# Seven products in shared PSUM banks, and an issue order written down for four engines

## The chip, the cores and the metric

The program runs on one core of a Trainium2 chip. A core has a matrix engine (TensorE, PE in the profile, with its weight loads as PEld), a vector engine (VectorE, DVE), an activation engine (ScalarE, ACT), a general engine (GpSimd, POOL) and an engine that here issues the DMAs (SyncE, SP). Each takes its instructions from a queue of its own, in order, and the engines wait for each other through semaphores. SBUF is the working memory, PSUM the eight banks that matmuls write to; POOL has no instruction here that reads PSUM.

The metric is the time of one execution on the device, in microseconds (us), lower being better.

## The reference

Two transformer-like layers over 512 latent tokens and 256 context tokens, width 1024. Each layer mixes tokens (layer 0: gated linear attention and a chunk MLP, layer 1: attention and a Fourier mix) and then runs a gated feed-forward block. Only this block matters for the change:

```python
def conv_ffn(h, w_up, conv_w, conv_b, w_down):
    t_len = h.shape[1]
    up = h @ w_up                                   # 1024 -> 2 x 2816
    gate, val = up[..., :D_FF], up[..., D_FF:]
    pad = CONV_W // 2
    gp = jnp.pad(gate, ((0, 0), (pad, pad), (0, 0)))
    gate_c = conv_b
    for j in range(CONV_W):                         # 3 taps along the tokens
        gate_c = gate_c + gp[:, j:j + t_len] * conv_w[j]
    return (jax.nn.silu(gate_c) * val) @ w_down
...
xl = xl + g2 * conv_ffn(modulate(xl, norm_ffn_w[l], sh2, sc2), ffn_w_up[l], ...)
```

In layer 0 it runs over latent and context tokens (768 columns), in layer 1 over the latent ones (512). All in float32.

## The kernel before

Features lie on the partitions, tokens in the columns. A float32 operand is kept as two tiles: `h`, the value rounded to the matmul's format by a cast on ACT, and `l`, the rest, from one subtraction on DVE or POOL. A product of two such pairs takes three matmuls (`mm3`, L499 to L503).

**Tiles and stages.** The hidden width 2816 is 22 tiles of 128. A tile needs 128 gate and 128 value features. Its result (`acts[i]`) goes into the second matrix product, "down", which runs in groups of tiles: layer 0 has groups of 3, 3, 3, 3, 3, 3, 4 tiles, layer 1 of 2, 4, 4, 4, 4, 4. In layer 0 the whole "down" of a group follows the first tile of the next group (24 x 6 matmuls of 512 or 256 columns). In layer 1 it is cut into chunks, one behind each tile (24 matmuls of 512 columns in the steady state, two output columns `m`). The last group's "down" follows all tiles (`down_last`). The first two tiles of a layer are computed plainly; tiles 2 to 21 by *products*.

**Products.** The tile's 2 x 2 block product (gate and value weights, each in two halves of the inner dimension, by the inputs, each in two halves of the tokens `n1` and `n2`) is made by seven products p0 to p6 instead of eight, each 12 matmuls of half the tokens: 384 columns in layer 0, 256 in layer 1. Their recombination is

- gate, first half: g1 = p0 + p5
- gate, second half: g2 = p0 + p1 + p3 + p2
- value, first half: u = p0 + p1 + p4 + p6
- value, second half: w = p0 + p1 + p3 + p4

Before, each product goes into a PSUM bank alone, and DVE makes one copy and seven adds out of PSUM (L1145 to L1162). There are eight banks under two tags, "mm" and "aux", four each; a tile takes two of each and uses three of them twice.

**Tail.** From gate, u and w: bias and middle tap (ACT, L1172, "bias step"), two shifted multiply-adds on DVE per token segment (L1174, L1176, "shifts"; layer 0 has two segments, so four), Silu (ACT, L1178), multiplication by u (POOL, L1179) and by w (DVE, L1180), then the pair for "down": cast (ACT, L1182) and subtraction (POOL, L1183). "Down" ends with the residual, one DVE instruction per segment that reads PSUM (L990).

**The weight stream** (`_Stream`, L292). Raw weights come by DMA on SP's queue. A unit of the look-ahead (`prep`) makes the pairs: for a plain or "down" chunk one cast (L490) and one subtraction (L492; POOL for most chunks); for a tile of products five units. Product 0, 5 and 6 take a raw quarter, 1, 2 and 3 need three sums on DVE first (L381 to L383), 4 one (L387); then a cast on ACT (L390) and a subtraction (L392) each, on DVE for the products in `PROD_ON_V`, else on POOL. `next`, called ahead of each product and each "down" chunk, emits the units that fit:

```python
def ready(self):
    ...
    own = PROD_OWN[int(self.order[i][0][2:])]
    return used + len([j for j in u if j not in own]) <= 6 and not self.own & set(u)

def next(self, key):
    ...                                  # the item before is no longer live
    while key not in self.hl:
        self.prep()
    while self.ready():
        self.prep()
    ...
```

Six tiles of the pool `whl` hold the prepared weights: one for a product, two for a "down" chunk; the products in `PROD_OWN` have buffers of another pool. Three buffers (tag "t2k") hold u, w and the sum for product 4; in layer 0 three others (tag "ada") hold gate, t1 and product 6's weights.

**What sets the order.** The framework's scheduler: it takes the instructions of all engines from a heap, by priorities and a planned time, and decides each engine's order as well as which buffer a tile gets. So the order in which the code emits is not the order in which an engine issues.

Of the kernel before, what the change touches and what calls it, by code (L numbers as in the profile page):

```python
# [11 lines left out]
F32 = mybir.dt.float32  # L12
# [4 lines left out]
ALU = mybir.AluOpType  # L17
# [32 lines left out]


def prod_order(layer, t):

    return PROD_FIRST if t == FF_PLAIN[layer] else PROD_USE

# [236 lines left out]
class _Stream:  # L292
# [4 lines left out]
    def __init__(self, nc, w, raw_pool, hl_pool, order, offs, split, last_pool, sums):  # L297
# [6 lines left out]
        while i < len(order):  # L304
            kind, t = order[i]
            if kind[:2] == "up" and FF_PLAIN[int(kind[2:])] <= t < NFF:
                for u in PROD_UNITS:
                    self.units.append((i, u))
                self.items += [(kind, t, j) for j in prod_order(int(kind[2:]), t)]
# [111 lines left out]
def backbone(ctx: ExitStack, tc, w, xt, ada, vec, cst, msk, rop, wst, bs, pew, out):  # L421
# [77 lines left out]
    def mm3(ps, a, b, first, last):  # L499

        T.matmul(ps, a[0], b[0], start=first, stop=False)  # L501
        T.matmul(ps, a[0], b[1], start=False, stop=False)  # L502
        T.matmul(ps, a[1], b[0], start=False, stop=last)  # L503


    bg = {"gla": deque(), "ada": deque(), "sum": deque()}
# [485 lines left out]
    def out_pass(key, nk, src, dst, gcol, each, chunks=None):  # L992

        per = 8 // nk
        for m in range(KD):
# [5 lines left out]
            ps = [bank("mm") for _ in d]  # L1001
# [24 lines left out]
    def ffn(layer, X, src, parts, late, down_last):  # L1026
# [106 lines left out]
        def up_products(t, gate):  # L1133
# [4 lines left out]
            def product(j, ps):  # L1138
                h, l = ws.next((f"up{layer}", t, j))
                for kk in range(4):  # L1140
                    mm3(ps[:, 0:nh], (h[:, kk * P:(kk + 1) * P], l[:, kk * P:(kk + 1) * P]), rhs[j][kk],
                        kk == 0, kk == 3)
                return ps[:, 0:nh]

            def add(o, a, b):  # L1145
                V.tensor_tensor(o, a, b, op=ALU.add)  # L1146

            b1, b2, b4, b3 = bank("mm"), bank("mm"), bank("aux"), bank("aux")
            u = tp.tile([P, nh], F32, tag="t2k", name="u")
            w_ = tp.tile([P, nh], F32, tag="t2k", name="w")  # L1150
            g1, g2, u, w_ = gate[:, n1], gate[:, n2], u[:], w_[:]
            todo = [((0,), lambda p: V.tensor_copy(g1, p[0])), ((0, 1), lambda p: add(u, g1, p[1])),
                    ((1, 3), lambda p: add(w_, u, p[3])), ((2, 3), lambda p: add(g2, w_, p[2])),
                    ((3, 4), lambda p: add(u, u, p[4])), ((3, 4), lambda p: add(w_, w_, p[4])),
                    ((1, 5), lambda p: add(g1, g1, p[5])), ((3, 4, 6), lambda p: add(u, u, p[6]))]
            banks = (b1, b2, b4, b3, b1, b2, b3)
            done = {}
# [639 lines left out]
```

## Time and profile before

| what | value |
|---|---|
| time, median of 3 runs | 1715.54 us (1711.6 to 1715.75) |
| the profiled execution's own time | 1715.11 us |
| its span, first to last instruction | 1713.3 us |
| PE busy | 1609.6 us (94%) |
| DVE busy | 1160.7 us (68%) |
| ACT busy | 684.8 us (40%) |
| POOL busy | 736.5 us (43%) |
| granted PE clock, mean | 0.989 |
| layer 0, tiles by products | 507 to 972 us |
| layer 1, tiles by products | 1354 to 1690 us |

The profile is of one execution. In a row of a group, the numbers are busy time in us, mean ns of one instruction, and the idle time of the engine before them with what ended it. A row of the waits has engine, line and releaser, then us in total, times and the longest. A row of the timeline has start, length, engine, line, and what it wrote and read. Names such as wp, kt, lt, slot and t are those of the program's tiles: wp is a product's prepared weight, wh and wl are those of a chunk, kt, lt and slot are pools. Matmuls overlap, so the distance between their starts is what one costs.

### The profile page before, as it was taken

To read this page: it belongs to the slowest core of one execution; us is meant where nothing else is said; L and a number is where in the kernel's file an instruction comes from. 1 tells how busy PE (TensorE), PEld (TensorE's weight loads), DVE (VectorE), ACT (ScalarE), POOL (GpSimd) and SP (SyncE) were. 2 spreads that over 40 slices of the span, in tenths; PEclk is the share of its full clock that TensorE was granted. 3 is DMA by queue.
4 is the path that set the end of the run, shared out by engine and by line. 5 is a ranking of instruction groups with operands and counts; after the bars stand their busy time and mean duration, and the time that the engine had idled before them with its cause. 6 is when DMAs were issued, how large, how long until landed. Compare 5 with 4: busy or idle time off the path is not lost.

```text
span 1713.3 us, 28274 instructions
## 1 busy us (share of the span) xinstructions
PE 1609.6 (94%) x11130; PEld 1423.2 (83%) x11130; DVE 1160.7 (68%) x2125; ACT 684.8 (40%) x1373; POOL 736.5 (43%) x456
## 2 busy tenths in 40 slices
PE   5999999989999999999999999989899989999999
PEld 4777777778999989889898888666799978888887
DVE  5337676752756756666566784777866788888884
ACT  4323333522453323233232453556654544343431
POOL 1221223344535656565565423411126355555551
PEclk9999999999999999999999999999999999999999
DMA  9353434323412122121221223633015222222222
GB/s 365 98 190 119 150 112 141 119 88 109 136 35 77 53 69 77 59 77 47 73 79 58 81 84 104 243 119 106 18 52 170 82 74 91 89 97 87 99 78 83
DMA packets 53205, 175.11 MB, mean 102 GB/s; under 512 B 5712, under 2 KB 7760, under 8 KB 53072
## 3 DMA queue, kind: packets, MB, share of 16 engines
q1 hardware_dynamic: 52208, 172.24, 30.8%
q8 instruction: 88, 1.44, 0.3%
q10 hardware_dynamic: 864, 1.07, 0.2%
q14 instruction: 45, 0.37, 0.1%
HBM read 171.18 MB, written 2.10 MB: 101 GB/s over the span
## 4 chain that ended last, share of the span: by engine, by line
PE 61%; DVE 21%; issue 5%; POOL 5%; ACT 4%; DMA 3%; ACTq 0%; DVEq 0%; SPq 0%; POOLq 0%
PE mm L501 14%; PE mm L502 14%; PE mm L503 14%; PE aux L501 3%; PE aux L502 3%; PE aux L503 3%; DVE wp L392 3%; PE aux L572 2%; POOL wl L492 2%; DMA raw<-in_w_dram 1%; DVE qk L832 1%; POOL wp L392 1%; DVE qk L830 1%; DVE kt L382 1%; PE aux L1105 1%
## 5 line engine op out<-in xcount | busy, mean ns | idle before, releaser
L492 POOL TENSOR_TENSOR wl<-raw,wh 128x1024 fp32r<-128x1024 f32 (+6 forms) x143 | 311.9, 2183 | 503.0 <-ACT wh L490 452.1
L490 ACT CAST wh<-raw 128x1024 fp32r<-128x1024 f32 (+5 forms) x155 | 146.4, 945 | 145.4 <-PE mm L502 75.9
L392 POOL TENSOR_TENSOR wp<-sum,wp 128x512 fp32r<-128x512 f32 x80 | 111.7, 1403 | 155.7 <-ACT wp L390 155.7
L501 PE MATMUL mm<-slot,wh 128*128 128x512 f32 (+1 forms) x480 | 163.7, 342 | 12.7 <-DVE xl L990 10.8
L502 PE MATMUL mm<-slot,wh 128*128 128x512 f32 (+1 forms) x480 | 163.0, 340 | 1.0 <-POOL slot L1183 0.7
L503 PE MATMUL mm<-slot,wl 128*128 128x512 f32 (+1 forms) x480 | 162.1, 338 | 0.0
L990 DVE SCALAR_TENSOR_TENSOR xl<-mm,mods,xl 128x512 f32<-128x512 f32 (+1 forms) x128 | 90.9, 712 | 96.9 <-PE mm L503 96.6
L392 POOL TENSOR_TENSOR wp<-raw,wp 128x512 fp32r<-128x512 f32 x80 | 113.7, 1429 | 67.5 <-ACT wp L390 67.5
L501 PE MATMUL mm<-xt,wh 128*128 128x256 f32 (+1 forms) x384 | 135.1, 354 | 0.2 <-ACT xt L641 0.2
L390 ACT CAST wp<-sum 128x512 fp32r<-128x512 f32 x100 | 60.8, 620 | 185.6 <-DVE sum L387 79.7
L502 PE MATMUL mm<-xt,wh 128*128 128x512 f32 (+1 forms) x384 | 129.8, 339 | 0.0
L503 PE MATMUL mm<-xt,wl 128*128 128x512 f32 (+1 forms) x384 | 129.7, 339 | 0.0
L501 PEld LDWEIGHTS mm<-slot,wh 128*128 128x128 f32 x480 | 90.7, 189 | 26.8 <-DVE xl L990 12.0
L501 PE MATMUL mm<-lt,wh 128*128 128x512 f32 (+2 forms) x308 | 107.1, 348 | 0.0
L503 PE MATMUL mm<-lt,wl 128*128 128x512 f32 (+2 forms) x308 | 106.6, 346 | 0.0
L502 PE MATMUL mm<-lt,wh 128*128 128x512 f32 (+2 forms) x308 | 106.6, 346 | 0.0
L502 PEld LDWEIGHTS mm<-slot,wh 128*128 128x128 f32 x480 | 91.1, 190 | 11.6 <-POOL slot L1183 1.1
L503 PEld LDWEIGHTS mm<-slot,wl 128*128 128x128 f32 x480 | 91.2, 190 | 10.4
L390 ACT CAST wp<-raw 128x512 fp32r<-128x512 f32 x100 | 61.8, 618 | 95.0 <-PE mm L502 36.5
L501 PEld LDWEIGHTS mm<-xt,wh 128*128 128x128 f32 x384 | 72.3, 189 | 26.3 <-issue 16.8
L1179 POOL TENSOR_TENSOR t<-t,u 128x384 f32<-128x384 f32 (+1 forms) x40 | 46.1, 1153 | 99.3 <-ACT t L1178 99.3
L501 PE MATMUL aux<-kt,wp 128*128 128x256 f32 x240 | 69.0, 288 | 19.7 <-DVE w L1146 19.7
(360 smaller groups left out, 4944.3 us busy)
## 6 DMA issues: line engine op xcount, KB each, us to landing
raw<-in_w_dram SPq DMA_DIRECT2D x162, 512.0 KB, 3.6
ada_t<-in_ada_dram SPq DMA_DIRECT2D x80, 512.0 KB, 4.7
raw<-in_w_dram SPq DMA_DIRECT2D x31, 384.0 KB, 3.1
wp<-in_w_dram SPq DMA_DIRECT2D x20, 512.0 KB, 4.6
kt<-in_ada_dram SPq DMA_DIRECT2D x16, 512.0 KB, 6.1
x<-in_xt_dram SPq DMA_DIRECT2D x8, 384.0 KB, 7.3
raw<-in_w_dram SPq DMA_DIRECT2D x10, 256.0 KB, 2.6
xl<-in_xt_dram SPq DMA_DIRECT2D x2, 1024.0 KB, 6.9
```

The source lines that it names most:

```text
L382: V.tensor_tensor(s2, s1, a11, op=ALU.subtract)
L390: S.copy(h, a)
L392: e.tensor_tensor(l, a, h.bitcast(F32), op=ALU.subtract)
L490: S.copy(h, raw)
L492: e.tensor_tensor(l, raw, h.bitcast(F32), op=ALU.subtract)
L501: T.matmul(ps, a[0], b[0], start=first, stop=False)
L502: T.matmul(ps, a[0], b[1], start=False, stop=False)
L503: T.matmul(ps, a[1], b[0], start=False, stop=last)
L572: T.matmul(ps[32 * q:32 * q + 32, :], sc_pad[:, k, :], t[:, j * 512:(j + 1) * 512], start=(k == 0), stop=(k == KD - 1))
L830: V.tensor_tensor(qa, qa, pick(FF[:], NT + m, [[2 * m, nb], [-(NT + m), 2], [0, m]]), op=ALU.mult)
L990: V.scalar_tensor_tensor(xs, ps, gate, xs, op0=ALU.mult, op1=ALU.add)
L1179: G.tensor_tensor(t1[:, n1], t1[:, n1], u, op=ALU.mult)
```

## The change

Four things, all in the tiles by products.

1. Three banks a tile instead of four (A and C of "mm", B of "aux"). Products that are added to each other accumulate in one bank, and ACT copies the bank out between them: p0, copy; p1 on top, copy; p3 on top; p2 on top, copy. p4, copy, and p6 on top. p5 alone. DVE keeps three adds out of PSUM; four copies are ACT's.
2. The order of the products is 0, 5, 1, 4, 3, 6, 2, that of the look-ahead's units 0, 5, (1, 2, 3), 4, 6. In layer 1 product 0's subtraction goes from DVE to POOL.
3. The tail becomes a generator of five steps. The first is emitted at the end of its tile, each further one at an `advance("tail")`: behind a column of "down", or between the next tile's products. What is left is drained at the end of the next tile.
4. From the first tile by products to the last "down" the code stands in a region `manual_schedule` for PE, ACT, DVE and POOL: in it each of these engines issues in the order in which the code emits. SP stays with the scheduler, as does the choice of buffers. The banks of "down" alternate between the two tags by output column.

```diff
-PROD_ON_V = ((2,), (0, 1, 2, 3))
+PROD_ON_V = ((2,), (1, 2, 3))
 PROD_OWN = ((6,), (0, 4, 5, 6))
-PROD_UNITS = ((0,), (1, 2, 3), (4,), (5,), (6,))
-PROD_USE = (0, 1, 2, 3, 4, 5, 6)
-PROD_FIRST = (0, 1, 2, 3, 4, 5, 6)
+PROD_UNITS = ((0,), (5,), (1, 2, 3), (4,), (6,))
+PROD_USE = (0, 5, 1, 4, 3, 6, 2)
...
-    def out_pass(key, nk, src, dst, gcol, each, chunks=None):
+    def out_pass(key, nk, src, dst, gcol, each, chunks=None, tags=("mm", "mm")):
...
-            ps = [bank("mm") for _ in d]
+            ps = [bank(tags[m % 2]) for _ in d]
...
-            def product(j, ps):
+            def product(j, ps, first=True, last=True):
                 h, l = ws.next((f"up{layer}", t, j))
                 for kk in range(4):
                     mm3(ps[:, 0:nh], (h[:, kk * P:(kk + 1) * P], l[:, kk * P:(kk + 1) * P]), rhs[j][kk],
-                        kk == 0, kk == 3)
+                        first and kk == 0, last and kk == 3, skip_group_check=True)
...
+            A, B, C = bank("mm"), bank("aux"), bank("mm")
+            pa, pb, pc = A[:, 0:nh], B[:, 0:nh], C[:, 0:nh]
...
+            product(0, A, last=False)
+            S.copy(u, pa)
+            advance("tail")
+            product(5, B)
+            V.tensor_tensor(g1, u, pb, op=ALU.add)
+            advance("tail")
+            product(1, A, False, False)
+            S.copy(u, pa)
+            advance("tail")
+            product(4, C, last=False)
+            S.copy(w_, pc)
+            advance("tail")
+            product(3, A, False, False)
+            V.tensor_tensor(w_, w_, pa, op=ALU.add)
+            product(6, C, False)
+            V.tensor_tensor(u, u, pc, op=ALU.add)
+            product(2, A, False)
+            S.copy(g2, pa)
             return u, w_
 
+        def tail(i, gate, u, w_):
...
+            S.activation(t1[:, 0:nw], gate[:, 0:nw], AF.Identity, bias=vcol("convb", layer * NFF + i), scale=cw(1))
+            yield
+            for c0, b, bc, n in merged:
+                V.scalar_tensor_tensor(t1[:, c0 + 1:c0 + n], gate[:, c0:c0 + n - 1], cw(0), t1[:, c0 + 1:c0 + n],
+                                       op0=ALU.mult, op1=ALU.add)
+                V.scalar_tensor_tensor(t1[:, c0:c0 + n - 1], gate[:, c0 + 1:c0 + n], cw(2), t1[:, c0:c0 + n - 1],
+                                       op0=ALU.mult, op1=ALU.add)
+            yield
+            S.activation(t1[:, 0:nw], t1[:, 0:nw], AF.Silu)
+            yield
+            G.tensor_tensor(t1[:, n1], t1[:, n1], u, op=ALU.mult)
+            V.tensor_tensor(t1[:, n2], t1[:, n2], w_, op=ALU.mult)
+            yield
+            a = acttile()
+            S.copy(a[:, 0, 0:nw], t1[:, 0:nw])
+            G.tensor_tensor(a[:, 1, 0:nw], t1[:, 0:nw], a[:, 0, 0:nw].bitcast(F32), op=ALU.subtract)
+            acts[i] = a
+
         plain = FF_PLAIN[layer]
+        order = ExitStack()
         for kind, i, *cs in seq:
+            if kind == "up" and i == plain:
+                ET = mybir.EngineType
+                order.enter_context(tc.manual_schedule(engines={ET.PE, ET.Activation, ET.DVE, ET.Pool}))
+            if kind == "down" and i == len(groups) - 1:
+                drain("tail")
+                order.close()
             if kind == "up" and i >= plain:
                 gate = t1tile()
                 u, w_ = up_products(i, gate)
...
+                drain("tail")
+                acts[i] = None
+                bg["tail"].append(tail(i, gate, u, w_))
+                advance("tail")
...
                     out_pass(f"down{layer}_{i}", n, pairs, xdst, lambda m, s: mods[layer][:, 40 + m, s:s + 1],
-                             lambda m: None, cs[0])
+                             lambda m: advance("tail"), cs[0], ("mm", "aux"))
```

More of the change, by code (lines that the diff above doesn't have):

```diff
@@ L497, in backbone, with mm3 @@
                  lambda l, n: sum_pool[l](n))
[L499 to L506, printed above, removed]
+    def mm3(ps, a, b, first, last, **kw):
+        T.matmul(ps, a[0], b[0], start=first, stop=False, **kw)
+        T.matmul(ps, a[0], b[1], start=False, stop=False, **kw)
+        T.matmul(ps, a[1], b[0], start=False, stop=last, **kw)
+    bg = {"gla": deque(), "ada": deque(), "sum": deque(), "tail": deque()}
     def advance(kind):
@@ L1141, in product @@
                     mm3(ps[:, 0:nh], (h[:, kk * P:(kk + 1) * P], l[:, kk * P:(kk + 1) * P]), rhs[j][kk],
-                        kk == 0, kk == 3)
[L1143 to L1157, printed above, removed]
-            for j in prod_order(layer, t):
-                done[j] = product(j, banks[j])
-                for need, f in [x for x in todo if all(k in done for k in x[0])]:
-                    f(done)
-                todo = [x for x in todo if not all(k in done for k in x[0])]
@@ L1163, in up_products @@
-            return u, w_
+                        first and kk == 0, last and kk == 3, skip_group_check=True)
+            A, B, C = bank("mm"), bank("aux"), bank("mm")
+            pa, pb, pc = A[:, 0:nh], B[:, 0:nh], C[:, 0:nh]
+            u = tp.tile([P, nh], F32, tag="t2k", name="u")[:]
+            w_ = tp.tile([P, nh], F32, tag="t2k", name="w")[:]
+            g1, g2 = gate[:, n1], gate[:, n2]
+            product(0, A, last=False)
+            S.copy(u, pa)
+            advance("tail")
@@ L1169, in ffn @@
                 u, w_ = up_products(i, gate)
-                t1 = t1tile()
-                cw = lambda j: vcol("convw", (layer * 3 + j) * NFF + i)
-                S.activation(t1[:, 0:nw], gate[:, 0:nw], AF.Identity, bias=vcol("convb", layer * NFF + i), scale=cw(1))
-                for c0, b, bc, n in merged:
-                    V.scalar_tensor_tensor(t1[:, c0 + 1:c0 + n], gate[:, c0:c0 + n - 1], cw(0), t1[:, c0 + 1:c0 + n],
-                                           op0=ALU.mult, op1=ALU.add)
-                    V.scalar_tensor_tensor(t1[:, c0:c0 + n - 1], gate[:, c0 + 1:c0 + n], cw(2), t1[:, c0:c0 + n - 1],
-                                           op0=ALU.mult, op1=ALU.add)
-                S.activation(t1[:, 0:nw], t1[:, 0:nw], AF.Silu)
-                G.tensor_tensor(t1[:, n1], t1[:, n1], u, op=ALU.mult)
-                V.tensor_tensor(t1[:, n2], t1[:, n2], w_, op=ALU.mult)
-                a = acttile()
-                S.copy(a[:, 0, 0:nw], t1[:, 0:nw])
-                G.tensor_tensor(a[:, 1, 0:nw], t1[:, 0:nw], a[:, 0, 0:nw].bitcast(F32), op=ALU.subtract)
-                acts[i] = a
+                drain("tail")
+                acts[i] = None
+                bg["tail"].append(tail(i, gate, u, w_))
+                advance("tail")
             elif kind == "up":
```

6 lines of the change are left out of this document (3 added, 3 removed).

## The prediction

> **What bounds the kernel now.** I read the page first, then the two stretches in which tiles are computed by products (layer 0 and layer 1), then what TensorE (PE) waits for in each, then one tile of layer 1.
>
> ```profile
> span 1713.3 us, 28274 instructions
> ```
> ```profile
> 507.00:972.00 465.00, 453.01 (x2569) 430.04 (x2567) 302.66 (x455) 153.73 (x223) 269.98 (x179) 1.00 0.23 69
> ...
> 1354.00:1690.00 336.00, 311.22 (x2133) 285.98 (x2132) 284.23 (x416) 136.24 (x216) 184.51 (x116) 0.99 0.26 87
> ```
> ```profile
> PE mm L501 <- DVE xl L990: 10.8, 6, 1.8
> ...
> PE aux L501 <- DVE w L1146: 19.7, 17, 2.4
> ```
> ```profile
> 1492.52:1509.70 17.18, 16.00 (x109) 14.60 (x108) 14.56 (x21) 6.96 (x11) 9.78 (x6) 1.00 0.27 92
> ```
>
> The columns of a window are its length, then busy time of PE, weight loads, DVE, ACT and POOL. PE is busy in 453 of 465 us and in 311 of 336 us: both stretches are close to PE's own time. What is left to win is small and has a name: in layer 0 PE waits 10.8 us, six times, once in each "down" group, for DVE's residual (L990); in layer 1 it waits 19.7 us, 17 times, because a bank of a product is still being read by DVE's add (L1146). One steady tile of layer 1 lasts 17.18 us, with PE busy 16.00 and DVE 14.56. So at most some 1.2 us a tile in layer 1 and 10.8 us in layer 0 are there to be had, together about 30 us. Since PE is full, the question is what the new order makes PE wait for.
>
> **The prices.** The first three fences show DVE, POOL and ACT at one moment of that tile (start, length, instruction), the fourth the groups, the last one product of layer 1 (12 matmuls, from its first to that of the next).
>
> ```profile
> 1474.55 0.68 DVE L392 TENSOR_TENSOR wp<-kt,wp 128x512 fp32r<-128x512 f32 x1
> 1475.26 0.69 DVE L381 TENSOR_TENSOR kt<-wp 128x512 f32<-128x512 f32 x1
> ...
> 1477.80 1.73 DVE L382 TENSOR_TENSOR kt<-kt,raw 128x512 f32<-128x512 f32 x1
> 1479.45 0.41 DVE L1146 TENSOR_TENSOR t<-t,mm 128x256 f32<-128x256 f32 x1
> ...
> 1481.48 0.74 DVE L1174 SCALAR_TENSOR_TENSOR t<-t,vt,t 128x511 f32<-128x511 f32 x1
> ```
> ```profile
> 1477.67 1.30 POOL L392 TENSOR_TENSOR wp<-sum,wp 128x512 fp32r<-128x512 f32 x1 [3.60 <-ACT wp L390]
> ```
> ```profile
> 1476.97 0.62 ACT L390 CAST wp<-sum 128x512 fp32r<-128x512 f32 x1 [3.85 <-DVE sum L387]
> 1477.50 0.61 ACT L390 CAST wp<-raw 128x512 fp32r<-128x512 f32 x1
> ```
> ```profile
> L490 ACT CAST wh<-raw 128x1024 fp32r<-128x1024 f32 x102 | 106.9, 1049 | 100.8 <-PE mm L502 63.7 <-issue 14.6 <-PE aux L503 14.4
> L492 POOL TENSOR_TENSOR wl<-raw,wh 128x1024 fp32r<-128x1024 f32 x90 | 223.9, 2489 | 359.5 <-ACT wh L490 338.3 <-PE aux L817 14.3 <-PE aux L503 3.3
> L1172 ACT ACTIVATE t<-t,vt 128x512 f32<-128x512 f32 x20 | 16.3, 817 | 34.1 <-DVE t L1146 34.1
> L1178 ACT ACTIVATE t<-t 128x512 f32<-128x512 f32 x20 | 12.6, 632 | 47.1 <-DVE t L1176 47.1
> L1179 POOL TENSOR_TENSOR t<-t,u 128x256 f32<-128x256 f32 x20 | 19.1, 957 | 65.4 <-ACT t L1178 65.4
> L1182 ACT CAST lt<-t 128x512 fp32r<-128x512 f32 x20 | 12.4, 620 | 22.0 <-POOL t L1179 19.6 <-DVE t L1180 2.4
> L711 ACT COPY fm<-aux 128x256 f32<-128x256 f32 x8 | 3.0, 374 | 24.6 <-PE aux L708 24.6
> ```
> ```profile
> 1455.10 0.36 PE L501 MATMUL mm<-lt,wp 128*128 128x256 f32 x1
> ...
> 1456.60 0.29 PE L501 MATMUL mm<-kt,wp 128*128 128x256 f32 x1
> ```
>
> The DVE subtraction at 1477.80 takes 1.73 us where the same shape alone takes 0.69: POOL's at 1477.67 runs until 1478.97, and only then does DVE's go on. DVE's add with a PSUM operand at 1479.45 keeps its 0.41 beside a busy POOL. So I let a DVE instruction with two SBUF inputs wait until POOL's current one ends, and the reverse. A handover between engines costs 0.08 (ACT's cast ends at 1477.59, POOL starts at 1477.67); casts on ACT start 0.53 apart. The new copy out of PSUM is in the program elsewhere: 0.37 for 256 columns.
>
> **Part by part.** Five of eight PSUM operations leave DVE, 5 x 0.41 = 2.05 us a tile in layer 1; four copies of 0.37 go to ACT, which has room. The subtraction for product 0 in layer 1 goes from DVE (0.68) to POOL (1.30). The alternating banks in "down" and the residuals' new place on DVE take the 10.8 us away. None of this is on PE; the matmuls stay 84 a tile. Weight loads stay where they were on SP's queue, which the region doesn't order, and a tile ahead of use (over 14 us, against the 3.6 us to landing of the last row below), so no DMA gets a price. What has one is that the order is now written: each engine takes what was emitted first, also when that waits. I followed the emission through the stream's look-ahead and found two loops.
>
> *Layer 1, one tile with its "down" chunk.* The look-ahead for the next tile's products 1, 2, 3, 4 is emitted before product 6, that for 6 before product 2; then the copy of g2; the tail's bias step; after the chunk's two columns the two shifts and Silu; then, before the next tile's product 0, the next down chunk's cast and subtraction; copy of product 0; the tail's multiplications; its cast after product 5; the copy of product 0+1; product 3, which accumulates onto the bank just copied; DVE's add of it. And only behind this add do DVE's sums of the next look-ahead stand. From the end of product 3, in us:
> - DVE: add 0.1 to 0.5; first sum behind POOL's running subtraction to 1.4, two more to 2.8; three subtractions and the sum for product 4 to 5.4.
> - ACT: cast for 4 to 6.1, for 6 to 6.6, copy of g2 to 6.9, bias step to 7.7.
> - DVE: the shift waits for POOL's subtraction for 6 (after that for 4: 6.2 + 1.30 + 1.30) until 8.7; two shifts to 10.1.
> - ACT: Silu to 10.8, down cast to 11.7. POOL: down subtraction, begun at 11.8, to 14.2, multiplication to 15.0.
> - ACT: the tail's cast to 15.6, the cast for 5 to 16.1, the copy to 16.4.
> - PE: product 3, 1.5 us: 18.0.
>
> (For the down subtraction I take 2.4, for the multiplication 0.8, a little under their means, as DVE is quiet there.) So a tile takes 18.0 us against 17.18: +0.8, for the 16 tiles from 6 to 21, +13 us. Without any wait between DVE and POOL the same loop is 16.9, -5 us in all; with one more POOL subtraction (1.30) in the way it is 19.3, +34. I take 18.0, since the rows show such waits at just these places. The layer's first four tiles, two of them without a chunk behind them, I leave at nothing: they are 4 of 20, and the loop is shorter there by the down cast and subtraction.
>
> *Layer 0.* The rows for its shapes, and PE's first two products:
>
> ```profile
> L990 DVE SCALAR_TENSOR_TENSOR xl<-mm,mods,xl 128x512 f32<-128x512 f32 x112 | 83.2, 745 | 86.5 <-PE mm L503 86.2
> ...
> L990 DVE SCALAR_TENSOR_TENSOR xc<-mm,mods,xc 128x256 f32<-128x256 f32 x64 | 30.2, 474 | 1.4 <-PE mm L503 1.4
> ...
> L1172 ACT ACTIVATE t<-t,vt 128x768 f32<-128x768 f32 x20 | 20.6, 1031 | 17.5 <-DVE t L1146 17.5
> L1106 ACT CAST slot<-aux 128x384 fp32r<-128x384 f32 x12 | 5.6, 479 | 7.3 <-PE aux L1105 7.3
> L1178 ACT ACTIVATE t<-t 128x768 f32<-128x768 f32 x20 | 16.9, 846 | 24.4 <-DVE t L1176 24.4
> ...
> L1182 ACT CAST slot<-t 128x768 fp32r<-128x768 f32 x20 | 16.7, 836 | 32.7 <-POOL t L1179 32.7
> ...
> L1179 POOL TENSOR_TENSOR t<-t,u 128x384 f32<-128x384 f32 x20 | 27.0, 1348 | 33.9 <-ACT t L1178 33.9
> ```
> ```profile
> 507.45 0.34 PE L501 MATMUL mm<-xt,wp 128*128 128x384 f32 x1
> ...
> 511.61 0.34 PE L501 MATMUL aux<-xt,wp 128*128 128x384 f32 x1
> ```
>
> Two products take 4.16 us, so product 1 may start 4.16 us after a tile does, if the copy of product 0 is done. After a down group (tiles 4, 7, 10, 13, 16, 19) the look-ahead for the tile's own products 1 to 4 and 6 is emitted just before its product 0, and DVE's sums stand behind the group's last residual. From the group's last matmul: two residuals to 1.2; three sums to 3.3; DVE's subtraction for 2 behind POOL's for 1 to 5.2; the sum for 4 behind POOL's for 3 to 7.0; casts for 4 and 6 to 8.2; copy of product 0 to 8.6 (384 columns: 0.48). PE stands 4.4 us; without DVE waiting for POOL 2.8. Six times: 26.4, or 16.8. In a tile that follows another directly, ACT has between P2's end and that copy: copy of g2 0.48, bias 1.03, cast for 4 0.62, and, since the copy's buffer is the one that held the sum for 4, POOL's subtraction 1.30, then 0.48, with five handovers 4.3: about no stall. One shift of DVE (0.6) twice, and in the second tile of a pair POOL's subtraction for 3 ahead of the sum, make it 1.3 and 2.4, 3.7 a pair. I take half, 1.9, for six pairs, and 0.6 for tile 3: 12. Layer 0: 26.4 + 12 - 10.8 = +28; ends +6 (16.8 - 10.8) and +39 (26.4 + 23.5 - 10.8).
>
> *The end of layer 0.* Its last tile's tail now follows product 2, and nothing of it can run ahead.
>
> ```profile
> 971.80 0.83 ACT L1182 CAST slot<-t 128x768 fp32r<-128x768 f32 x1 [1.50 <-POOL t L1179]
> ```
> ```profile
> 966.78 0.39 PE L501 MATMUL mm<-slot,wh 128*128 128x512 f32 x1
> ```
> ```profile
> raw<-in_w_dram SPq DMA_DIRECT2D x162, 512.0 KB, 3.6
> ```
>
> Today the cast ends 5.9 us after the products do (972.63 - 966.78). Then: copy 0.48, bias 1.03, four shifts 2.4, Silu 0.85, multiplication 1.35, cast 0.84, handovers 0.6: 7.5, +1.7. In layer 1 the last chunk of "down" covers it: 0, and 2 if it doesn't.
>
> **The sum**, against the profiled execution's own 1715.11 us (span 1713.3 and 1.8 around it; the median shown is 1715.54, so no correction): +28 +13 +2 = +43, **1758 us**. The ends: +6 -5 +0 = 1716, and +39 +34 +4 = 1792.
>
> [...] PE's clock after a wait of about 2 us:
>
> ```profile
> 616.90:619.50 2.60, 0.78 (x5) 0.52 (x4) 2.60 (x4) 0.00 (x0) 2.60 (x2) 1.00 0.67 202
> 619.50:623.30 3.80, 3.80 (x15) 3.22 (x14) 0.92 (x2) 0.00 (x0) 0.50 (x1) 0.55 0.48 138
> ```
>
> After one of the six waits for the residual the granted clock was 0.55 for 3.8 us, a loss of 3.8 x 0.45 = 1.7 us; one such loss is no more than the six waits hold now, so the sum leaves it out. [...]
>
> **Rivals.**
> - *The copies come early enough* (faster). If ACT ends the copy of product 0+1 before product 4 does, PE never waits: then layer 1 goes to PE's busy 16.0 (16 x 1.2 = -19) and layer 0 loses its 10.8, with +2 at its end: **1687**. For it: DVE is busy 14.56 of 17.18 now and gets 2 us back, and the six waits do go. Against: it needs the loop under 16.0, and it is 16.9 even with no wait for POOL. It decides where the tail's cast, which stands before that copy, is done 2 us sooner than I have it.
> - *DVE and POOL hardly wait for each other* in the new order: the lower ends, **1716**. Against it: the 1.73.
> - *The clock drops* at each of layer 0's six stalls: 6 x 1.7 = +10, **1768**.
> - *A buffer decides.* In layer 0 gate, t1 and product 6's weights share three buffers. If the next gate takes the free one, the cast for 6 waits for the shifts (2.4 and up to 1.8 of POOL), in 13 tiles: +30 to +55, **1800**. That the order doesn't do what it says could be only in this way, through buffers, which the scheduler still hands out.
>
> **How the numbers follow.** The forecast gets 0.57, the clock 0.08, the buffer 0.05, hardly any waits 0.08, early copies 0.22. 0.3% is 5.1 us, about what a measurement here can tell from no change; the forecast's lower edge and the third case share the 0.06 of "same" and a little of "faster". Slower 0.70, same 0.06, faster 0.24. The forecast's own range is 1725 to 1790; with the upper half of the early copies, which may come true in one layer only, 1692 to 1790.
>
> **What would show it.** PE's waits should name ACT's copies (product 1 after a down group, about 4 us; product 3 in layer 1, about 1.6 us, product 1 about 1), a steady tile of layer 1 should last 18 us, the residual's waits should be gone, and POOL's multiplication should start right after its down subtraction. A tile of 16 us with PE unbroken, or waits that name DVE, would prove the loops wrong.

## The result and the profile after

The changed kernel takes 1781.41 us (median of 4 runs, 1778.65 to 1782.07); the kernel before, on the same chip, 1715.64 us (1711.6 to 1716.6). The ratio is 1.0385, with a 95% interval of 1.0372 to 1.0397: slower by 66 us. Its profiled execution has a span 67.0 us longer than the one before (1713.3).

```profile
span 1780.3 us, 28105 instructions
```

The line numbers are now those of the changed kernel: L495 to L497 are the three matmuls of a step; L1146, L1152, L1155 and L1162 are ACT's copies after product 0, after product 1, after product 4 and of g2; L1149, L1158 and L1160 DVE's three additions; L1169 to L1184 the tail; L384 and L386 the casts and subtractions of the look-ahead, L375 to L377 and L381 its sums, L484 and L486 the cast and subtraction of a down chunk, L984 the residual.

I first look at the two stretches, from the first to the last matmul of a product. The window view (length, then busy PE, weight loads, DVE, ACT and POOL, with the number of instructions, then PE's granted clock), the kernel before:

```profile
507.45:966.60 459.15, 447.40 (x2544) 425.66 (x2544) 298.93 (x449) 152.24 (x220) 268.21 (x177) 1.00 0.23 68
...
1354.32:1681.69 327.37, 302.59 (x2094) 278.78 (x2092) 279.09 (x409) 132.87 (x213) 182.22 (x114) 0.99 0.27 88
```

The same stretches after the change, and one steady tile of layer 1:

```profile
507.03:1014.44 507.41, 464.33 (x2544) 438.14 (x2544) 276.51 (x351) 182.53 (x299) 260.74 (x178) 0.96 0.20 61
...
1402.91:1747.16 344.25, 307.52 (x2090) 282.42 (x2088) 195.05 (x292) 155.83 (x291) 178.26 (x133) 0.98 0.25 84
...
1610.81:1628.59 17.78, 16.01 (x110) 14.55 (x109) 9.79 (x16) 8.03 (x15) 9.35 (x8) 1.00 0.27 91
```

Layer 0 is 48.3 us longer and layer 1 16.9; together that is 65 of the 67 us. Both parts split in two. PE stands still longer: 43.1 us in place of 11.8 in layer 0 (length less busy time), 36.7 in place of 24.8 in layer 1. And PE takes longer for the same 2544 matmuls: 464.3 us in place of 447.4, at a granted clock of 0.96, and 4.9 us more in layer 1. DVE did get its time back, 84 us of it in layer 1 alone; nothing came of that.

What PE waited for (line and engine waited for: us in all, times, longest), layer 0 and then layer 1:

```profile
PE mm L495 <- ACT u L1146: 40.2, 19, 4.0
```
```profile
PE mm L495 <- ACT u L1152: 22.8, 18, 2.6
PE mm L495 <- ACT u L1146: 13.9, 17, 3.3
```

The waits for the residual and for DVE's additions are gone, and every large wait now names a copy of a shared bank by ACT. What makes a copy late is read from the queues. Layer 0, a tile behind a down group: PE (product 5's first matmul, and product 1's with the wait before it and its cause), then DVE, POOL and ACT:

```profile
800.98 0.33 PE L495 MATMUL aux<-xt,wp 128*128 128x384 f32 x1
...
807.18 0.44 PE L495 MATMUL mm<-slot,wp 128*128 128x384 f32 x1 [3.96 <-ACT u L1146]
```

```profile
798.74 0.75 DVE L984 SCALAR_TENSOR_TENSOR xl<-aux,mods,xl 128x512 f32<-128x512 f32 x1 [1.98 <-PE aux L497]
...
799.79 0.68 DVE L375 TENSOR_TENSOR sum<-raw 128x512 f32<-128x512 f32 x1
...
802.74 1.12 DVE L386 TENSOR_TENSOR wp<-sum,wp 128x512 fp32r<-128x512 f32 x1 [0.81 <-ACT wp L384]
803.78 1.74 DVE L381 TENSOR_TENSOR sum<-raw 128x512 f32<-128x512 f32 x1
```
```profile
802.02 2.96 POOL L386 TENSOR_TENSOR wp<-sum,wp 128x512 fp32r<-128x512 f32 x2 [9.45 <-ACT wp L384]
```
```profile
801.32 1.85 ACT L384 CAST wp<-sum 128x512 fp32r<-128x512 f32 x3 [13.23 <-DVE sum L376]
805.62 0.62 ACT L384 CAST wp<-sum 128x512 fp32r<-128x512 f32 x1 [2.46 <-DVE sum L381]
806.14 0.61 ACT L384 CAST wp<-raw 128x512 fp32r<-128x512 f32 x1
806.66 0.47 ACT L1146 COPY u<-mm 128x384 f32<-128x384 f32 x1
```

Product 5 starts at 800.98, so product 0 is finished at about 801; its copy begins at 806.66, because five casts stand ahead of it on ACT, the fourth of which waits for DVE's sum for product 4, which waits beside POOL. And layer 1, in the tile above, ACT, POOL, and DVE's first shift:

```profile
1612.37 0.63 ACT L1177 ACTIVATE t<-t 128x512 f32<-128x512 f32 x1 [2.42 <-DVE t L1174]
1612.91 1.03 ACT L484 CAST wh<-raw 128x1024 fp32r<-128x1024 f32 x1
1613.85 0.36 ACT L1146 COPY u<-mm 128x256 f32<-128x256 f32 x1
...
1617.13 0.62 ACT L1183 CAST lt<-t 128x512 fp32r<-128x512 f32 x1 [2.40 <-POOL t L1179]
...
1618.18 0.36 ACT L1152 COPY u<-mm 128x256 f32<-128x256 f32 x1
```
```profile
1614.02 2.39 POOL L486 TENSOR_TENSOR wl<-raw,wh 128x1024 fp32r<-128x1024 f32 x1 [3.08 <-ACT wh L484]
1616.37 0.74 POOL L1179 TENSOR_TENSOR t<-t,u 128x256 f32<-128x256 f32 x1
```
```profile
1609.99 1.50 DVE L1172 SCALAR_TENSOR_TENSOR t<-t,vt,t 128x511 f32<-128x511 f32 x1 [1.03 <-ACT t L1169]
```

The first copy stands behind Silu and the down cast; the second behind the tail's cast, which waits for POOL's multiplication, which stands behind the down subtraction. The shift takes 1.50 us where the prediction's row has 0.74: it starts while POOL still makes a subtraction (from 1609.64, 1.30 us long).

The longer matmuls are for the most part a loss of clock. First the window behind the stall above; then two waits of 2.2 us in other tiles, each with two windows of 3.41 us, the one that ends near the wait's end and the next (the granted clock is the third number from the end):

```profile
807.50:810.92 3.42, 3.42 (x12) 3.42 (x11) 0.22 (x1) 0.67 (x2) 3.42 (x4) 0.50 0.57 187
```
```profile
841.71 0.69 PE L495 MATMUL mm<-slot,wp 128*128 128x384 f32 x1 [2.16 <-ACT u L1146]
```
```profile
838.23:841.64 3.41, 1.32 (x8) 1.00 (x6) 3.37 (x4) 1.64 (x4) 2.13 (x3) 1.00 0.37 106
841.64:845.05 3.41, 3.34 (x10) 3.34 (x11) 3.02 (x5) 1.41 (x3) 1.18 (x1) 0.50 0.34 110
```
```profile
685.27 0.44 PE L495 MATMUL mm<-slot,wp 128*128 128x384 f32 x1 [2.17 <-ACT u L1146]
```
```profile
681.21:684.62 3.41, 1.89 (x11) 1.57 (x10) 3.38 (x4) 1.76 (x3) 2.13 (x2) 1.00 0.23 68
684.62:688.03 3.41, 2.76 (x16) 2.77 (x17) 3.10 (x4) 1.27 (x3) 1.78 (x2) 1.00 0.32 72
```

In layer 0 of this trace the granted clock is either 1.00 or 0.50, and a slow stretch lasts 3.41 us or 6.83. There is one behind each of the six stalls of 4.0 us (behind two of them, from 568.58 and from 886.04, the longer), and one behind three of the six waits of 2.0 to 2.2 us. The wait at 841.71 (2.16 us; PE busy 1.32 of the 3.41 us up to 841.64) is followed by one. The wait at 685.27 is as long (2.17 us; PE busy 1.89 and 2.76 us in its two rows), and it costs no clock. So the length of a wait did not decide it alone; what did, these runs do not show.

A slow window of 3.41 us loses 3.41 x 0.5 = 1.7 us. Layer 0 has eleven, a stretch of 6.83 us counted as two: eight behind the six stalls of 4.0 us and three behind the six waits of 2.0 to 2.2 us. That is 18.8 us, of which 1.7 fall into the waits themselves, where nothing is lost. The kernel before has one, so some 15.4 of the 16.9 us are clock; the rest I did not trace.

### The profile page after: what moved, and what is told of

It is laid out like the page before. It is cut to its first block, busy times and chain, and to the rows that moved or that the text cites. A ratio compares the mean times of both kernels' runs of the same rounds, so it can differ in the third digit from the quotient of the medians.

```text
span 1780.3 us, 28105 instructions
## 1 busy us (share of the span) xinstructions
PE 1630.1 (92%) x11130; PEld 1438.5 (81%) x11130; DVE 1050.8 (59%) x1905; ACT 738.8 (41%) x1533; POOL 724.8 (41%) x476
## 5 line engine op out<-in xcount | busy, mean ns | idle before, releaser
L486 POOL TENSOR_TENSOR wl<-raw,wh 128x1024 fp32r<-128x1024 f32 (+6 forms) x143 | 301.8, 2112 | 608.4 <-ACT wh L484 564.3
L386 POOL TENSOR_TENSOR wp<-sum,wp 128x512 fp32r<-128x512 f32 x80 | 110.5, 1388 | 255.3 <-ACT wp L384 255.2
L484 ACT CAST wh<-raw 128x1024 fp32r<-128x1024 f32 (+5 forms) x155 | 145.8, 942 | 106.3 <-PE mm L496 72.3
L495 PE MATMUL mm<-kt,wp 128*128 128x256 f32 x400 | 117.6, 294 | 36.7 <-ACT u L1152 22.8
L386 POOL TENSOR_TENSOR wp<-raw,wp 128x512 fp32r<-128x512 f32 x100 | 136.7, 1379 | 18.0 <-ACT wp L384 18.0
L495 PE MATMUL mm<-xt,wh 128*128 128x256 f32 (+1 forms) x384 | 135.3, 353 | 0.0
L384 ACT CAST wp<-sum 128x512 fp32r<-128x512 f32 x100 | 60.0, 620 | 177.6 <-DVE sum L376 124.0
L1158 DVE TENSOR_TENSOR w<-w,mm 128x384 f32<-128x384 f32 (+1 forms) x40 | 19.5, 487 | 188.6 <-PE mm L497 187.8
L984 DVE SCALAR_TENSOR_TENSOR xl<-mm,mods,xl 128x512 f32<-128x512 f32 (+1 forms) x84 | 58.5, 699 | 121.2 <-PE mm L497 121.0
L497 PE MATMUL mm<-xt,wl 128*128 128x256 f32 (+1 forms) x384 | 129.4, 339 | 0.0
L495 PE MATMUL mm<-slot,wp 128*128 128x384 f32 x240 | 90.4, 377 | 41.7 <-ACT u L1146 40.2
L496 PE MATMUL mm<-slot,wh 128*128 128x512 f32 (+1 forms) x336 | 113.0, 336 | 1.3 <-POOL slot L1184 0.9
L496 PE MATMUL mm<-kt,wp 128*128 128x256 f32 x400 | 113.9, 285 | 0.0
L497 PE MATMUL mm<-kt,wp 128*128 128x256 f32 x400 | 113.9, 285 | 0.0
L495 PE MATMUL mm<-slot,wh 128*128 128x512 f32 (+1 forms) x336 | 112.8, 337 | 1.0 <-ACT slot L1183 1.0
L495 PEld LDWEIGHTS mm<-kt,wp 128*128 128x128 f32 x400 | 77.5, 194 | 44.6 <-ACT u L1152 26.6
L497 PE MATMUL mm<-slot,wl 128*128 128x512 f32 (+1 forms) x336 | 112.5, 335 | 0.0
L495 PEld LDWEIGHTS mm<-xt,wh 128*128 128x128 f32 x384 | 72.4, 189 | 25.9 <-issue 16.8
L495 PEld LDWEIGHTS mm<-slot,wp 128*128 128x128 f32 x240 | 50.3, 210 | 49.7 <-ACT u L1146 46.3
L496 PE MATMUL mm<-slot,wp 128*128 128x384 f32 x240 | 86.9, 362 | 0.0
L497 PE MATMUL mm<-slot,wp 128*128 128x384 f32 x240 | 86.8, 362 | 0.0
```

The source lines that it names most:

```text
L384: S.copy(h, a)
L386: e.tensor_tensor(l, a, h.bitcast(F32), op=ALU.subtract)
L484: S.copy(h, raw)
L486: e.tensor_tensor(l, raw, h.bitcast(F32), op=ALU.subtract)
L495: T.matmul(ps, a[0], b[0], start=first, stop=False, **kw)
L496: T.matmul(ps, a[0], b[1], start=False, stop=False, **kw)
```

## Experiments

My theory after reading the two profiles: PE waits for ACT's copies since, in the written order, the look-ahead and the tail stand ahead of them on three queues; and the clock that these stalls cost comes on top. The rival: the shared banks themselves, which leave one product's time for a copy, cost it in any order. "After" below is the changed kernel; stretches are lengths from the first to the last product.

**The order left to the scheduler.**

```
-                order.enter_context(tc.manual_schedule(engines={ET.PE, ET.Activation, ET.DVE, ET.Pool}))
+                pass
```

> The changed kernel without the written order: banks, copies, product order and the tail's five steps as changed, but the scheduler orders all engines again. Written-order theory: the loss is the order's, so PE's waits for ACT's copies fall from 79 us in all to under 20 us and the time comes to 1705 to 1730 us. Rival, shared banks: the copies between products of one bank are themselves too late, whoever orders them; the waits for ACT's copies stay above 50 us and the time above 1755 us.

Measured: 1737.45 us, ratio to the kernel before 1.0139 (1.012 to 1.0158); layer 0 480.3, layer 1 325.0. That lies between the two: 44 of the 66 us go, 22 remain, with these waits in layer 0:

```profile
PE mm L495 <- ACT u L1152: 25.8, 13, 2.4
```

So neither theory holds alone. In layer 1 the scheduler gets below the kernel before (327.4); in layer 0 a copy is still late, the one between products 1 and 3.

**Only ACT left to the scheduler.**

```
-engines={ET.PE, ET.Activation, ET.DVE, ET.Pool}
+engines={ET.PE, ET.DVE, ET.Pool}
```

> The changed kernel with the written order for PE, DVE and POOL only; ACT is ordered by the scheduler. Written-order theory: PE waits because ACT's copies stand behind casts in ACT's own queue, so with ACT free the waits for copies fall by more than half (79 us to under 40 us) and the time to 1725 to 1750 us. Rival: the order of DVE and POOL (sums behind the residual, multiplication behind the down subtraction) is what makes it late; ACT can gain little by slipping the copies ahead, and the time stays at 1765 us or more.

Measured: 1822.27 us, 1.0625 (1.061 to 1.0641), a miss: slower still, layer 0 520.7 and layer 1 367.4. Layer 1's largest wait, then ACT and POOL in one of its tiles:

```profile
PE mm L495 <- ACT u L1146: 42.8, 16, 3.4
```
```profile
1659.37 0.62 ACT L1183 CAST lt<-t 128x512 fp32r<-128x512 f32 x1 [2.41 <-POOL t L1179]
1659.89 0.36 ACT L1146 COPY u<-mm 128x256 f32<-128x256 f32 x1
```
```profile
1655.64 2.83 POOL L486 TENSOR_TENSOR wl<-raw,wh 128x1024 fp32r<-128x1024 f32 x1
1658.44 0.90 POOL L1179 TENSOR_TENSOR t<-t,u 128x256 f32<-128x256 f32 x1
```

The scheduler put the tail's cast ahead of the first copy. The cast waits for POOL's multiplication, and POOL, whose order stayed written, does the down subtraction first. So ACT's own queue is not the whole fault: what its instructions wait for on POOL counts as well, and with the order of POOL and DVE still written, freeing ACT did not mend it. Freeing POOL or DVE alone was not tried.

**Product 0's look-ahead behind its copy.** The look-ahead that stands ahead of product 0 is emitted behind the copy and the tail's step that follows it. Written so, the sum for product 4 in layer 0 needs a buffer of its own (sbuf tile "s4"), or DVE would wait for a multiplication that stands behind it.

```
-                h, l = ws.next((f"up{layer}", t, j))
+                h, l = ws.next((f"up{layer}", t, j), j != 0)
...
             S.copy(u, pa)
             advance("tail")
+            ws.ahead()
...
-            return [tp.tile([P, 512], F32, tag="t2k", name="sum")[:]]
+            return [l0c.tile([P, 512], F32, tag="s4", name="sum")[:]]
```

> The changed kernel with one move in the written order: the look-ahead of product 0 is emitted behind the copy of product 0 and the tail's step there, no longer ahead of product 0; in layer 0 the sum for product 4 gets a buffer of its own, which the move needs. Written-order theory: in layer 0 after a down group product 1 waits 0.5 us for its own weights instead of 4.1 for the copy (6 x 3.6 = -22, and the clock's loss behind it, some -8), in the other tiles the copy no longer stands behind two casts (-15); in layer 1 the multiplication comes ahead of the down subtraction and the copy ahead of the down cast, so a tile falls from 17.8 to about 16.2 us (-25): 1705 to 1725 us in all. Rival: the loops only move their wait to the next product, and the time stays at 1760 us or more.

Measured: 1743.83 us, 1.0171 (1.0156 to 1.0187), 38 us below after; layer 0 484.1, layer 1 331.7. Layer 0's waits are now (mm3 stands five lines lower here)

```profile
PE mm L502 <- POOL wp L386: 10.7, 20, 0.7
PE mm L500 <- ACT wp L384: 9.1, 13, 0.9
```

The stalls at product 1 are gone from layer 0. What replaces them is smaller: the weights of the next products now come late, since their casts and subtractions begin later. Each is under 1 us, but some of the clock stays lost in layer 0, too (granted clock 0.98 over its stretch, 0.96 in after): at 872.54 and 873.90 PE waits 0.90 and 0.74 us, and from 874.93 to 878.13 the matmuls start 0.32 us apart, in place of 0.17. So layer 0 lost 23 us where the theory had 45. Layer 1 lost 12.5 of the 25 expected, since 23.9 us of waits for product 0's copy stayed there. That is why the time stopped short of 1705 to 1725.

**The buffer alone.** The last of the three edits above, on the changed kernel.

> The changed kernel with one thing else: in layer 0 the sum for product 4 has a buffer of its own, so that it no longer waits for one of the three that u and w rotate through. It tells how much of the 38 us of the run with product 0's look-ahead behind its copy came from the buffer that it needed. Theory 'the place of the look-ahead is the cause': the six stalls of 4.1 us behind a down group stay, only the 3 us of pairs of layer 0 shrink: 1770 to 1779. Rival 'the buffer is the cause': DVE's copy chain no longer waits for the multiplications, the stalls at product 1 go: 1740 to 1755.

Measured: 1773.97 us, 1.0362 (1.0333 to 1.0392): the theory's range. The buffer is worth some 7 us by the times, but 4 by the ratios to the kernel before, whose intervals overlap; the place of product 0's look-ahead is worth the other 30 or so.

**Matmuls in the stall.** In the six tiles of layer 0 behind a down group, 19 matmuls whose result nobody reads stand between products 5 and 1.

```
             product(5, B)
+            if layer == 0 and t in (4, 7, 10, 13, 16, 19):
+                F = bank("aux")
+                for _ in range(19):
+                    T.matmul(F[:, 0:nh], eye[0][:], rhs[0][0][0], start=True, stop=True)
```

> The changed kernel with 19 more matmuls of 384 columns (3.3 us), whose result nobody reads, behind product 5 of the six tiles of layer 0 that follow a down group, where PE stands 4.1 us. Clock theory: the stall drops PE's clock and the matmuls after it run slow; with PE kept busy the granted clock there stays at 1.00 and the time falls by 6 x 1.3 to 1.8 us, 8 to 11 us, to about 1771 us, though the copies come no earlier. Rival: the matmuls behind the stall are slow for another reason; the time stays at 1781 us or rises.

Measured: 1774.09 us, 1.0344 (1.0328 to 1.0359), 7.3 us below after. Layer 0:

```profile
509.19:1008.44 499.25, 476.26 (x2659) 450.17 (x2658) 276.90 (x351) 182.30 (x299) 260.54 (x178) 0.98 0.21 63
```

114 more matmuls of 0.174 us each are 19.8 us of work more, and the stretch is 8.2 us shorter. PE's time for the matmuls that count is 476.3 - 19.8 = 456.5 in place of 464.3. So the clock that the six stalls cost is real, 7.8 us net. All eight slow windows behind them are gone. Five others stay, behind five of the six waits of 2.0 to 2.2 us, where the changed kernel had three; those waits are as long as before (2.00 to 2.17 us in both).

**The written order alone.** Region, tail and alternating down banks of the change; products, banks and DVE's eight operations of the kernel before, with a step of the tail behind each of the first four products.

```
-PROD_USE = (0, 5, 1, 4, 3, 6, 2)
+PROD_USE = (0, 1, 2, 3, 4, 5, 6)
...
+            banks = (b1, b2, b4, b3, b1, b2, b3)
...
+            for j in PROD_USE:
+                done[j] = product(j, banks[j])
+                if j < 4:
+                    advance("tail")
```

> The other half of the change alone: the written order of the four engines and the tail's steps behind the next tile's first four products stay; the recombination is that of the kernel before (seven products in banks of their own, eight DVE operations, its order and units of the products, product 0's low half on DVE). Without the written order the shared banks cost 22 us. Theory 'the order costs by itself, whatever it orders': the sums and subtractions of the look-ahead stand ahead of each product's own DVE operation, so banks and weight operands come late anyway: 1750 to 1765, about the 44 us by which the change exceeds those 22. Rival 'the two only hurt together', because the first copy is read within one product and a bank of its own isn't needed again for four: waits of PE in the loops under 20 us in all and 1705 to 1720.

Measured: 1754.73 us, 1.0243 (1.0227 to 1.0258), as the first theory had it; layer 0 466.0, layer 1 352.0. Layer 1's waits, and DVE's queue at one of them (product 6 starts at 1609.94, on the addition at 1609.38):

```profile
PE aux L495 <- DVE w L1140: 40.7, 18, 4.4
```
```profile
1604.10 0.89 DVE L375 TENSOR_TENSOR kt<-wp 128x512 f32<-128x512 f32 x1
...
1607.36 2.11 DVE L386 TENSOR_TENSOR wp<-kt,wp 128x512 fp32r<-128x512 f32 x3
1609.38 0.41 DVE L1140 TENSOR_TENSOR w<-u,aux 128x256 f32<-128x256 f32 x1
```

Without any shared bank the same thing happens on another engine: 5.3 us of look-ahead, written down ahead of the 0.41 us that frees a bank.

**The recombination alone.** Shared banks and copies, the order left to the scheduler, and the tail written whole behind its tile.

```
-                order.enter_context(tc.manual_schedule(engines={ET.PE, ET.Activation, ET.DVE, ET.Pool}))
+                pass
...
                 bg["tail"].append(tail(i, gate, u, w_))
-                advance("tail")
+                drain("tail")
```

> The recombination alone (shared banks, copies, new order and units of the products, alternating banks in down), with the order left to the scheduler and the tail written whole behind its tile, as in the kernel before. The run without the written order, but with the tail in steps between the next tile's products, stood at 1737 us, with 25.8 us of waits at product 3 in layer 0. Theory 'the copies of the shared bank A cost that, whatever the tail does': product 3 goes on waiting for ACT's copy of products 0 and 1, 1732 to 1742, that is 35 to 45 above the old recombination with alternating banks (1697.6). Rival 'the tail's place in the program was it': ACT's copies go ahead of the tail's steps, waits under 10 us, 1705 to 1718.

Measured: 1741.14 us, 1.0151 (1.0133 to 1.017); layer 0 481.9, layer 1 326.6; the theory's range. Layer 0's wait, and ACT and DVE at one of them, where product 3 starts as the copy ends:

```profile
PE mm L495 <- ACT u L1152: 25.7, 13, 2.4
```
```profile
745.80 0.83 ACT L1183 CAST slot<-t 128x768 fp32r<-128x768 f32 x1 [0.97 <-POOL t L1179]
746.54 0.47 ACT L1152 COPY u<-mm 128x384 f32<-128x384 f32 x1
```
```profile
741.21 2.17 DVE L1174 SCALAR_TENSOR_TENSOR t<-t,vt,t 128x511 f32<-128x511 f32 x2
743.87 0.55 DVE L1149 TENSOR_TENSOR t<-u,aux 128x384 f32<-128x384 f32 x1 [0.48 <-DVE t L1174]
```

The copy overwrites u, which DVE's addition of g1 has to read first, and that addition comes behind the tail's shifts, until 744.42. What ends last, though, is the tail's cast ahead of the copy on ACT, which waits for POOL's multiplication. The tail's place in the program makes no great difference (1737 or 1741). A second buffer, so that the copy need not wait for that addition, was not tried; so this run does not show that the shared banks would cost as much in every order, only that they do in the scheduler's.

**The alternating banks alone.** The kernel before with one small part of the change: successive column groups of "down" take banks of "mm" and "aux" in turn.

```
-            ps = [bank("mm") for _ in d]
+            ps = [bank(tags[m % 2]) for _ in d]
```

> The kernel before with the one small part of the change that takes a wait away: the groups of a down pass alternate between the two sets of banks. In the trace before, PE waits six times in layer 0, 10.8 us in all, for the residual additions of DVE, 1.8 us each. Theory 'that part alone is worth its waits': these six waits go and nothing takes their place, 1703 to 1708. Rival 'DVE is what is late, not the bank': the residuals come behind the look-ahead's sums on DVE either way, and the next product waits instead, 1712 to 1717.

Measured: 1697.59 us, 0.9908 (0.989 to 0.9926), 16 us below the kernel before and better than both theories. Layer 0:

```profile
507.58:950.09 442.51, 442.51 (x2544) 424.74 (x2544) 298.62 (x449) 152.28 (x220) 268.60 (x177) 1.00 0.23 71
```

PE is busy for the whole of it. Against the kernel before, 11.8 us of waits are gone, and PE is busy 4.9 us less for the same 2544 matmuls: 16.6 us together. Little of that is clock. The kernel before has one slow window in layer 0, behind one of the six waits:

```profile
619.86:623.27 3.41, 3.41 (x13) 2.93 (x12) 0.56 (x2) 0.00 (x0) 0.14 (x1) 0.50 0.53 154
```

The two traces compared matmul by matmul, from start to start, give 12.4 us for the six waits (2.07 each; the 1.8 of the wait rows begins only at the end of the matmul before), 2.3 for five shorter delays in the down groups, and some 1.7 for the slow window. The theory had counted the 10.8 alone.

This is the proper base for the parts of the change, since all of them hold these banks: the recombination alone costs 1741 - 1698 = 43 us, the order alone 57, both 84. (By the ratios to the kernel before on each chip it is 42, 57 and 82.)

**And a bank of its own for product 6.**

```
-            b1, b2, b4, b3 = bank("mm"), bank("mm"), bank("aux"), bank("aux")
+            b1, b2, b4, b3, b5 = bank("mm"), bank("mm"), bank("aux"), bank("aux"), bank("mm")
...
-            banks = (b1, b2, b4, b3, b1, b2, b3)
+            banks = (b1, b2, b4, b3, b1, b2, b5)
```

> The kernel before with two banks changed: the groups of a down pass alternate between the two sets of banks (the run of that alone stands at 1697.6 us), and product 6 gets a bank of its own in place of product 3's. What waits are left there in layer 1 are 19.6 us in 17 places, PE for DVE's addition of product 3 into w, at product 6 that would overwrite it: 1.25 us in the tile looked at. Theory 'only the bank is late': these waits go and the tail, which comes after that addition anyway, hides in the down pass: 1678 to 1683. Rival 'DVE is what is late': its additions come no earlier, the tail's end or the next tile's weights come late in their place, 1693 to 1698.

Measured: 1696.26 us, 0.9891 (0.9874 to 0.9908); layer 1 326.5 in place of 327.5. That is no gain over the run before it, a miss for the theory, and the rival's case: the wait moved to product 4, which waits for DVE's copy of product 0.

```profile
PE mm L501 <- DVE t L1152: 25.4, 14, 3.6
```

This speaks for DVE as what is late in layer 1 of the old recombination; a bank of its own for product 4 as well was not tried.

**The tail one step later in layer 1.** On the kernel with product 0's look-ahead behind its copy, of which layer 1 had kept 23.9 us of waits at product 1.

```
-                             lambda m: advance("tail"), cs[0], ("mm", "aux"))
+                             lambda m: advance("tail") if layer == 0 or m % 2 == 0 else None, cs[0], ("mm", "aux"))
```

> On the kernel with product 0's look-ahead behind its copy (and the buffer for the sum): in layer 1 the tail takes one step fewer in the two down passes between tiles, so that Silu is queued on ACT behind the copy of product 0, and no longer ahead of it. That kernel stands 1.41 us per tile at product 1 in layer 1, on a copy that starts when Silu has ended, and Silu waits 2.4 us for DVE's second shift. Theory 'the tail's own chain (copy g2, bias step, two shifts, Silu) is too long for the time that is left': the wait goes, a steady tile takes 16.0 to 16.4 us in place of 17.1, layer 1 loses 10 to 17 us: 1727 to 1734. Rival 'the engines behind set the loop': the wait moves to product 3 or to a weight operand, the tile keeps 16.9 us or more: 1740 or more.

Measured: 1759.23 us, 1.0271 (1.0253 to 1.0288), 15 us slower than without it: layer 1 346.7 in place of 331.7. The theory missed; it is the rival's case, a wait at product 3 and a time above 1740. The waits of layer 1, and ACT at one of them:

```profile
PE mm L500 <- ACT w L1161: 29.2, 15, 2.4
```
```profile
1613.46 0.62 ACT L1189 CAST lt<-t 128x512 fp32r<-128x512 f32 x1 [3.24 <-POOL t L1185]
1613.98 0.36 ACT L1161 COPY w<-mm 128x256 f32<-128x256 f32 x1
```

The wait at product 1 did go. One step later, though, the tail's cast stands ahead of the copy of w, waiting for POOL.

**The cast behind that copy too.** On the kernel just above:

```
             S.copy(u, pa)
-            advance("tail")
+            if layer == 0:
+                advance("tail")
             product(4, C, last=False)
```

> On the kernel whose tail in layer 1 is one step later: the cast of the activation, the tail's last step, is queued on ACT behind the copy of w (after product 4) and no longer ahead of it. That kernel stands 29.2 us in 15 places at product 3, on the copy of w, which starts when the cast has ended, and the cast waits 3.2 us for POOL's multiplication, behind the down weights' subtraction. Theory 'each copy is late by what is queued ahead of it on ACT, and by nothing else': the wait goes, layer 1 loses 20 to 29 us of its 346.7, total 1730 to 1739. Rival 'some engine's loop is as long as the tile': the wait turns up at another product, and layer 1 keeps 335 us or more, total 1747 or more.

Measured: 1737.41 us, 1.0133 (1.0111 to 1.0155); layer 1 326.5, 20.2 us less than the run above. That is at the edge of what the theory said: the wait for the copy of w went, and one of 21.9 us stayed behind it, at product 3, for the copy after product 1. Layer 0 has the same code in both and was 4.7 us shorter (479.4 in place of 484.1), with PE busy 457.7 us in place of 462.4 for the same matmuls and a granted clock of 0.99 in place of 0.98, so that part of the gain is not the edit's. Layer 1 is now where the kernel before has it, though DVE is busy 225.9 us in it in place of 279.1. None of the written orders came below the kernel before; the versions that did are the old recombination with alternating banks.

## Why the prediction was right, and where it was off

The forecast, 1758 us, was slower for the reasons it gave; the time is 23 us higher and inside the range.

- *The loop of layer 1.* Forecast 18.0 us a tile, measured 17.78. The chain of the working holds step by step: in the tile above, counted from the end of the product 3 before it, Silu ends at 10.7 (forecast 10.8), the down cast at 11.6 (11.7), POOL's multiplication at 14.8 (15.0), the tail's cast at 15.4 (15.6), the copy at 16.2 (16.4). The waits of a steady tile are 0.56 us at product 1 and 1.21 at product 3; forecast about 1 and about 1.6. The stretch grew by 16.9 us, not 13, and not quite where the sum has it. The 14 steady tiles from 7 to 20 gave 9.0 (0.64 each), the last tile 2.1. Tile 6 alone gave 5.5, with a wait of 3.3 us at product 1 and two slow windows of the clock. The first four tiles, left at nothing, gave 0.4.
- *The six stalls of layer 0.* Forecast 4.4 us each, measured 4.0, with the chain as worked out: residuals, sums, subtraction, the sum for product 4 beside POOL, casts, copy. Moving this look-ahead behind the copy removed the stalls.
- *The pairs of layer 0.* Here a term was mis-sized. The working gave 3.7 us a pair and then took half without a row for it. The trace has 0.55 us (at 824.16) and 2.0 to 2.2 (2.16 at 841.71) by PE's waits, 2.7 a pair: 16.0 us for six pairs in place of 11.4. From start to start of the matmuls a pair costs 3.3, so the full 3.7 was nearer than its half.
- *The clock.* The step that failed: "one such loss is no more than the six waits hold now, so the sum leaves it out". The prediction took the loss behind one residual wait for that behind each of the six; the trace before has a slow window behind only one of them. So the term is 1.7 us before and, with eleven slow windows, 18.8 after: most of the 16.9 us by which the matmuls of layer 0 took longer. The rival had the price right, 1.7 us, and the number of places wrong, six for eleven. Eight of the eleven are behind the six stalls; three of the six waits of 2.0 to 2.2 us cost clock as well.
- *What was removed.* The 10.8 us of residual waits are gone, as said. The alternating banks by themselves are worth 16 us, as shown above: mostly waits, counted in full, and 1.7 of clock.
- *The end of layer 0.* Forecast +2; the time between the two stretches went from 387.7 to 388.5 us, +0.8.
- *The rivals.* Early copies (1687): in no run with shared banks did all of ACT's copies come early enough, with a written order or without. Hardly any waits between DVE and POOL (1716): DVE's 1.74 us for the sum for product 4, 0.69 alone, and 1.50 for the shift, 0.74 alone, show the wait again. A buffer that decides (1800): no wait of PE points at it; the sum's buffer was worth 4 to 7 us.

In sum: waits +31.3 and longer matmuls +16.9 in layer 0 make 48 where I had 28; 17 in layer 1 where I had 13; 1 at the end where I had 2. Both terms of layer 0 that were too small erred the same way, and the range, 1725 to 1790, was wide enough to hold them.

What stays open: how the change's products and copies would do with every piece of look-ahead and tail placed behind the copies in layer 0 as well; the last wait there, for weights that come 0.5 to 0.7 us late on average, was not tried away. Why two of the slow stretches of layer 0 lasted 6.83 us where the others lasted 3.41 is open, too, and why waits of one length cost clock in some places and not in others.

## What to carry to other kernels

An accumulator shared by several products with a copy in between turns that copy into a deadline one product long: list what stands ahead of it on its engine, and what each of these waits for on the other engines, before writing an order down. Price a stall of the matmul engine from start to start of its matmuls, and look at the granted clock behind it: in layer 0, 31.3 us more of waits brought some 15 us of lost clock with them. And try the smallest part of a change alone: the alternating banks, a few lines, were the gain, while the rest cost 84 us.

## What I had not expected of the hardware

What a wait cost in clock was not the same from one place to the next. In layer 0 of the changed kernel the granted clock was 0.50 for eleven times 3.41 us, 1.7 us lost each time, eight times at the six stalls of 4.0 us and three times behind waits of 2.0 to 2.2 us, of which there are six. Two waits of the same length, 2.2 us, cost 1.7 us or nothing, and in the run with product 0's look-ahead moved the matmuls behind two waits of 0.90 and 0.74 us ran at about half their pace for 3.2 us. The same code of layer 0 came out 4.7 us apart in two runs, at a granted clock of 0.98 and 0.99. Filling the long stalls with matmuls that nobody reads made the kernel 7.3 us faster.
